# Embedding: two weight halves loaded together, and where their splits stand in ScalarE's queue

## The chip, the core and the metric

One NeuronCore of a Trainium2 chip runs the kernel. Its engines are TensorE (PE, matmuls), VectorE (DVE), ScalarE (ACT), GpSimd (POOL) and SyncE (SP), which issues nearly all of the DMAs. Each engine works through its own queue in order and waits on semaphores. The metric is the device time of one execution, in microseconds (us), as a median of several runs.

## What is computed

The reference is one layer of a hybrid encoder on 1024 tokens of 1024 channels in float32: an input layer norm, a gated-delta-net and a forgetting-attention group that read one combined projection, an output projection, an MLP, and between them residuals with layer norms. The part that the change touches is small, the per-layer embedding:

```python
ff = jnp.square(jax.nn.relu(h @ w_up[i])) @ w_down[i]
ple = (p[i] @ w_ple[i]) * jax.nn.sigmoid(h @ w_ple_gate[i] + b_ple_gate[i])
h = _layer_norm(ALPHA * h + ff + ple, ln2_g[i], ln2_b[i])
```

`p` has 1024 rows of 256 values and `w_ple` is 256 x 1024. Only the product `p @ w_ple` is made in the stage looked at here.

## The kernel before

Each float32 operand of a product is split in two parts that the matmul takes: `hi`, a rounded copy that ACT casts (`nc.scalar.copy`), and `lo`, the difference that DVE makes (`split_lo`, line 53). A product is then three matmuls, hi x hi, hi x lo and lo x hi, in one PSUM bank.

The kernel starts with the embedding because it needs nothing but inputs. `p` is loaded in two parts of 512 KB (`pt[:, 0:4]` and `pt[:, 4:8]`, lines 227 and 239). `w_ple` is loaded in two halves of 512 columns, 512 KB each, by `load_ple(n)` (line 229), which also issues the half's cast on ACT (line 234) and its difference on DVE (line 235). `ple_prep(half)` (line 262) transposes one part of `p` on PE, eight 128x128 transposes into two banks; ACT copies each bank into `pth` and DVE takes the difference into `ptl`. `ple_mm(t, n)` (line 272) makes one group of six matmuls for row group `t` and weight half `n` into a bank of a pool of three (`pj`), ACT evacuates the bank with a factor 0.5 (line 279), and SP stores the result in `ple_spill`. The order in the code is: transposes of the first part of `p`, four groups with half 0, transposes of the second part, four groups with half 1, then the eight groups of the second part.

In the same first stretch ACT and DVE split eight tiles of the value projection's weights (`load_wv`, tile `wvr`, lines 246 to 251, four buffers), a narrow tile `wv_s` is cast on DVE (line 284), and DVE makes the layer norm of the rows of `x` (`ln_rows`, line 133), three tiles of which are in flight. After the embedding PE goes through the eight row tiles: it transposes each normalised tile (`to_act`, line 151) and multiplies it with the value weights (line 309).

The order of instructions in each engine's queue is not that of the code. A planner runs the program through its own estimates of durations and landings, and on each engine gives the next place to the instruction that is ready by these estimates and stands earliest in the code. `tc.issue_after(ins)` pins what is traced in its block, as far as it runs on the engine of `ins`, behind `ins` in that engine's queue; instructions of other engines get no such edge. It adds no semaphore.

Of the kernel before, what the change touches and what calls it, by code (L numbers as in the profile page):

```python
# [32 lines left out]
def _sl(i, n=P):  # L33
    return slice(i * n, (i + 1) * n)
# [3 lines left out]
def tile_block(ctx: ExitStack, tc: tile.TileContext, x, p, ln_in_g, ln_in_b, w_in, conv_w, a_log, dt_bias,  # L38
               gdn_norm_g, b_f, fox_norm_g, w_out, ln1_g, ln1_b, w_up, w_down, w_ple, w_ple_gate,
               b_ple_gate, ln2_g, ln2_b, out):  # L40
    nc = tc.nc
    PS = bass.MemoryType.PSUM
    x, p, out = x[0], p[0, 0], out[0]
# [9 lines left out]
    def split_lo(eng, lo, src, hi):  # L53
        eng.tensor_tensor(out=lo, in0=src, in1=hi.bitcast(F32), op=ALU.subtract)  # L54
# [111 lines left out]
    def pj(name):  # L166

        return psd.tile([P, 512], F32, tag="pj", name=name)

    def sm(name):  # L170
        return psx.tile([P, 512], F32, tag="sm", name=name)
# [40 lines left out]
    with tc.tile_pool(name="start", bufs=2, reuse_waits="tile") as stp:  # L212
# [6 lines left out]
        def load_x(t):  # L219
            xts[t] = stp.tile([P, D], F32, tag="x", name=f"x{t}", bufs=3)  # L220
            nc.sync.dma_start(out=xts[t], in_=x[_sl(t), :])
# [7 lines left out]
        def load_ple(n):  # L229

            w = [wpool.tile([P, 2, 512], dt, tag=tag, name=f"{tag}_ple{n}")
                 for tag, dt in (("w_raw", F32), ("w_hi", F32R), ("w_lo", F32R))]
            nc.sync.dma_start(out=w[0], in_=w_ple[:, _sl(n, 512)].rearrange("(k q) c -> q k c", q=P))
            nc.scalar.copy(out=w[1], in_=w[0])
            split_lo(nc.vector, w[2], w[0], w[1])
            return w[1:]

        wpl = [load_ple(0)]
        nc.sync.dma_start(out=pt[:, 4:8], in_=pv[:, 4:8])
        load_x(0)  # L240
        wpl.append(load_ple(1))
        nc.gpsimd.dma_start(out=gb, in_=ln_in_g.partition_broadcast(P))
        nc.gpsimd.dma_start(out=bb, in_=ln_in_b.partition_broadcast(P))
        wvs = stp.tile([P, NK, 8], F32, name="wv_s", bufs=1)
# [17 lines left out]
        def ple_prep(half):  # L262
            for k in range(2):
                ps = sm("ps_pT")
                for i in range(4):
                    nc.tensor.transpose(ps[:, _sl(i)], pt[:, half * 4 + i, _sl(k)], ident)
                hi = pth[:, k, _sl(half, 512)]
                nc.scalar.copy(out=hi, in_=ps)
                lo = nc.vector.tensor_tensor(out=ptl[:, k, _sl(half, 512)], in0=ps, in1=hi.bitcast(F32), op=ALU.subtract)
            return lo.ins  # L270

        def ple_mm(t, n):
            so = stp.tile([P, 512], F32, tag="po", name="ple_o", bufs=5)
            ps = pj("ps_ple")
            wh, wl = wpl[n]
            for k in range(2):
                for wi, (aa, w) in enumerate(((pth, wh), (pth, wl), (ptl, wh))):
                    nc.tensor.matmul(ps, aa[:, k, _sl(t)], w[:, k], start=(k == 0 and wi == 0), stop=(k == 1 and wi == 2))
            nc.scalar.mul(out=so, in_=ps, mul=0.5)
            nc.sync.dma_start(out=ple_rows[t, :, _sl(n, 512)], in_=so)  # L280

        prep0 = ple_prep(0)
        with tc.issue_after(prep0):
            nc.vector.tensor_copy(out=wv_hi[:, :, 520:528], in_=wvs)
            split_lo(nc.vector, wv_lo[:, :, 520:528], wvs, wv_hi[:, :, 520:528])
        for t in range(4):
            ple_mm(t, 0)
        ple_prep(1)
        for t in range(4):
            ple_mm(t, 1)  # L290
        for n in range(2):
            for t in range(4, 8):
                ple_mm(t, n)
        for col in (512,):
            ahead[col] = proj_w(col)
        for t in range(NT):
# [8 lines left out]
            for n in range(2):  # L305
                ps = pj(f"psv{t}")
# [4 lines left out]
                cs, w = slice(264 * n, min(264 * n + 264, 512)), (264, 248)[n]  # L311
# [16 lines left out]
        ps = sm("ps_cols")  # L328
# [540 lines left out]
    n = len(steps)  # L869
# [117 lines left out]
    for t in range(NT):  # L987
# [6 lines left out]
        for n in range(2):  # L994
            ps = early.get((t, n))
            if ps is None:
                ps = pj("ps_mix")
# [423 lines left out]
    for js in ((0, 1), (2,), (3,)):  # L1421
        w = P * len(js)
# [13 lines left out]
        for j in js:  # L1436
            t = 4 + j
# [37 lines left out]
```

## Time and profile before

| | us |
|---|---|
| median of 3 runs (1410.28 to 1414.26) | 1412.11 |
| the profiled execution | 1411.87 |
| its span, first to last instruction | 1410.1 |
| PE busy | 1375.8 |
| DVE busy | 1084.5 |
| ACT busy | 559.3 |

The profile is of one execution. Start times are us from the first instruction. An entry in square brackets in a timeline is the idle time of the engine before the row, and what ended it. A time to landing runs from the issue of a DMA to its last byte. Matmul ends are modelled, so the steps between the starts of matmuls are a better measure than their durations.

### The profile page before, as it was taken

What the parts mean: (1) busy time and instruction counts of PE and PEld (TensorE: products, weight loads), DVE (VectorE), ACT (ScalarE), POOL (GpSimd) and SP (SyncE); (2) the same over time, 40 slices, a digit from 0 to 9 for tenths busy, and PEclk for the clock granted to TensorE, in tenths of its full rate; (3) what the DMA queues carried; (4) which work ended last, traced back from release to release, by engine and by line L of the source; (5) the groups of instructions that cost most, each with busy time, mean ns of one, the idle gap of its engine ahead of it and who ended that gap; (6) DMA issues with size and microseconds to landing.
All of it is one profiled execution on the core that took longest, in us unless ns stands there. A gap on an engine that the chain in (4) does not pass through costs nothing.

```text
span 1410.1 us, 20582 instructions
## 1 busy us (share of the span) xinstructions
PE 1375.8 (98%) x7342; PEld 1165.8 (83%) x7342; DVE 1084.5 (77%) x2273; ACT 559.3 (40%) x1044; POOL 15.4 (1%) x32
## 2 busy tenths in 40 slices
PE   7999999999999999999989999999999999999997
PEld 5997888988898887777889888888888888888885
DVE  6968899578566888968988766777666898748867
ACT  5323443243226767721133333333333444555421
POOL 1000000000000000000000000000000000000000
PEclk9999999999999999999999999999999999999999
DMA  9825434445478765234666744444446893334342
GB/s 304 282 104 180 150 83 116 146 157 149 127 190 199 172 150 166 68 133 168 214 215 207 237 137 153 157 160 147 148 131 228 315 342 111 97 97 125 117 134 83
DMA packets 193470, 232.74 MB, mean 165 GB/s; under 512 B 41638, under 2 KB 121687, under 8 KB 193367
## 3 DMA queue, kind: packets, MB, share of 16 engines
q1 hardware_dynamic: 187750, 226.69, 51.4%
q10 hardware_dynamic: 5232, 3.67, 1.0%
q8 instruction: 58, 0.95, 0.3%
q0 software_dynamic: 384, 1.06, 0.2%
q14 instruction: 46, 0.37, 0.1%
HBM read 155.29 MB, written 76.09 MB: 164 GB/s over the span
## 4 chain that ended last, share of the span: by engine, by line
PE 51%; DVE 3%; DMA 3%; issue 1%; SPq 0%; ACT 0%; DVEq 0%; ACTq 0%
PE ps_uP L1208 22%; PE ps_db L1328 9%; PE ps_da L1328 9%; PE ps_gP L1075 4%; PE ps_mix L954 3%; PE ps_db L1433 3%; DMA r<-t_spill 1%; DVE h L51 1%; PE ps_tr L961 1%; DMA h<-h_spill 0%; DMA wo_raw<-in_w_out_dram 0%; DMA hb<-h_spill 0%; DMA gA<-in_w_ple_gate_dram 0%; DMA h_spill<-h 0%; DVE gv L51 0%
## 5 line engine op out<-in xcount | busy, mean ns | idle before, releaser
L1208 PE MATMUL ps_uP<-T,uS 128*128 128x512 f32 x576 | 133.5, 390 | 0.0
L1208 PEld LDWEIGHTS ps_uP<-T,uS 128*128 128x128 f32 x576 | 108.1, 188 | 23.0
L1298 ACT CAST rh<-rr 128x512 fp32r<-128x512 f32 x112 | 69.9, 624 | 138.4 <-PE ps_db L1328 49.4
L54 DVE TENSOR_TENSOR rl<-rr,rh 128x512 fp32r<-128x512 f32 x112 | 77.1, 689 | 61.2 <-ACT rh L1298 22.3
L1208 PE MATMUL ps_uP<-B,uA 128*128 128x512 f32 x384 | 92.4, 396 | 0.0
L1208 PEld LDWEIGHTS ps_uP<-B,uA 128*128 128x128 f32 x384 | 72.2, 188 | 17.4
L954 PE MATMUL ps_mix<-wo,act_hi 128*128 128x512 f32 x256 | 81.7, 396 | 0.3 <-ACT act_hi L834 0.3
L207 PE MATMUL g<-act_hi,in_hi 128*128 128x512 f32 x192 | 75.5, 393 | 0.0
L207 PE MATMUL g<-act_hi,in_lo 128*128 128x512 f32 x192 | 75.3, 392 | 0.0
L207 PE MATMUL g<-act_lo,in_hi 128*128 128x512 f32 x192 | 74.9, 390 | 0.0
L54 DVE TENSOR_TENSOR uA<-uraw,uA 128x512 fp32r<-128x512 f32 x48 | 33.2, 691 | 47.8 <-ACT uA L1203 47.8
L1298 ACT CAST rl<-B 128x512 fp32r<-128x512 f32 x96 | 59.7, 623 | 24.5 <-PE ps_db L1328 11.5
L1203 ACT CAST uS<-wS 128x512 fp32r<-128x512 f32 x64 | 39.5, 624 | 73.0 <-issue 48.2
L54 DVE TENSOR_TENSOR ql<-B,rl 128x512 fp32r<-128x512 f32 x96 | 65.8, 686 | 0.3
L54 DVE TENSOR_TENSOR ptl<-ps_pt,pth 128x512 fp32r<-128x512 f32 (+2 forms) x96 | 51.1, 552 | 6.7 <-ACT pth L782 6.4
L954 PEld LDWEIGHTS ps_mix<-wo,act_hi 128*128 128x128 f32 x256 | 47.3, 188 | 10.1 <-DVE wo L54 0.6
L782 ACT CAST pth<-ps_pt 128x512 fp32r<-128x512 f32 (+2 forms) x96 | 44.4, 479 | 26.1 <-PE ps_pt L780 24.9
L51 DVE SCALAR_TENSOR_TENSOR cv<-g,hcw,cv 128x511 f32<-128x511 f32 (+2 forms) x72 | 52.8, 737 | 1.7 <-ACT cv L414 1.4
L764 ACT ACTIVATE s<-s,m 128x128 f32<-128x128 f32 (+3 forms) x64 | 49.9, 780 | 8.5 <-DVE m L761 7.8
L1328 PE MATMUL ps_db<-rl,rh 128*128 128x512 f32 x192 | 51.3, 389 | 0.0
L1328 PE MATMUL ps_db<-ql,rh 128*128 128x512 f32 x192 | 51.3, 389 | 0.0
L1328 PE MATMUL ps_db<-rl 128*128 128x512 f32 x192 | 51.3, 389 | 0.0
(358 smaller groups left out, 3586.0 us busy)
## 6 DMA issues: line engine op xcount, KB each, us to landing
uraw<-in_w_up_dram SPq DMA_DIRECT2D x32, 512.0 KB, 4.6
B<-in_w_down_dram SPq DMA_DIRECT2D x32, 512.0 KB, 5.1
rr<-rS SPq DMA_DIRECT2D x64, 256.0 KB, 2.6
in_raw<-in_w_in_dram SPq DMA_DIRECT2D x24, 512.0 KB, 4.3
rr<-rA SPq DMA_DIRECT2D x48, 256.0 KB, 2.8
h_spill<-h SPq DMA_DIRECT2D x16, 512.0 KB, 3.5
rA<-ub SPq DMA_DIRECT2D x32, 256.0 KB, 2.2
rS<-da SPq DMA_DIRECT2D x32, 256.0 KB, 2.1
```

What stands on the lines that cost most here:

```text
L51: nc.vector.scalar_tensor_tensor(out=o, in0=a, scalar=s, in1=b, op0=op0, op1=op1)
L54: eng.tensor_tensor(out=lo, in0=src, in1=hi.bitcast(F32), op=ALU.subtract)
L207: mm = nc.tensor.matmul(ps, w[:, k, :], a[n][:, :, k], start=(k == 0 and wi == 0), stop=(k == NK - 1 and wi == 2))
L764: nc.scalar.activation(out=s[:, :W], in_=s[:, :W], func=AF.Exp, bias=m[:, i:i + 1], scale=-1.0, accum_out=pairs[h // 2][2][:, r, j:j + 1])
L782: nc.scalar.copy(out=hi, in_=pt[:, :kn])
L954: nc.tensor.matmul(ps, a[t // 4][:, t % 4, k], w, start=(k == 0 and wi == 0), stop=(k == NK - 1 and wi == 2))
L1075: nc.tensor.matmul(ps[j // 2][:, j % 2], B[b][s][k][:, _sl(j)], a[w][:, k], start=(first and j % 2 == 0 and k == 0 and wi == 0), stop=(j % ...
L1203: nc.scalar.copy(out=hi, in_=a[s])
L1208: nc.tensor.matmul(ps[p], w[:, k], B[t][b][k], start=(chain is None and k == 0 and wi == 0), stop=(k == 3 and wi == 2), skip_group_check=c ...
L1298: nc.scalar.copy(out=hi, in_=src)
L1328: nc.tensor.matmul(ps[j], rs[x][:, _sl(j)], qs[y], start=(not chain and c == 0 and wi == 0), stop=(c == NP - 1 and wi == 2), skip_group_ch ...
L1433: nc.tensor.matmul(b[j], rs[x][:, i, _sl(j - js[0])], Q[c0 + i][y], start=(c0 == 0 and i == 0 and wi == 0), stop=(c0 + i == NP - 1 and wi ...
```

## The change

`load_ple` only loads now; a new `split_ple(n)` casts and subtracts. Both halves are loaded one behind the other, ahead of the second part of `p` and of the first tile of `x`. The split of half 0 is traced behind the first `ple_prep` and its cast is pinned in ACT's queue behind the second copy of the transposed `p` (`hi0`). The split of half 1 is traced behind the first four groups, its cast pinned behind the third evacuation (`o[2]`). The differences on DVE get no pin of their own. The same instructions run on the same data.

```diff
--- before.py
+++ after.py
@@ -231,14 +231,15 @@
             w = [wpool.tile([P, 2, 512], dt, tag=tag, name=f"{tag}_ple{n}")
                  for tag, dt in (("w_raw", F32), ("w_hi", F32R), ("w_lo", F32R))]
             nc.sync.dma_start(out=w[0], in_=w_ple[:, _sl(n, 512)].rearrange("(k q) c -> q k c", q=P))
-            nc.scalar.copy(out=w[1], in_=w[0])
-            split_lo(nc.vector, w[2], w[0], w[1])
-            return w[1:]
-
-        wpl = [load_ple(0)]
+            return w
+
+        def split_ple(n):
+            nc.scalar.copy(out=wpl[n][1], in_=wpl[n][0])
+            split_lo(nc.vector, wpl[n][2], wpl[n][0], wpl[n][1])
+
+        wpl = [load_ple(n) for n in range(2)]
         nc.sync.dma_start(out=pt[:, 4:8], in_=pv[:, 4:8])
         load_x(0)
-        wpl.append(load_ple(1))
         nc.gpsimd.dma_start(out=gb, in_=ln_in_g.partition_broadcast(P))
         nc.gpsimd.dma_start(out=bb, in_=ln_in_b.partition_broadcast(P))
         wvs = stp.tile([P, NK, 8], F32, name="wv_s", bufs=1)
@@ -265,26 +266,31 @@
                 for i in range(4):
                     nc.tensor.transpose(ps[:, _sl(i)], pt[:, half * 4 + i, _sl(k)], ident)
                 hi = pth[:, k, _sl(half, 512)]
-                nc.scalar.copy(out=hi, in_=ps)
+                last_hi = nc.scalar.copy(out=hi, in_=ps)
                 lo = nc.vector.tensor_tensor(out=ptl[:, k, _sl(half, 512)], in0=ps, in1=hi.bitcast(F32), op=ALU.subtract)
-            return lo.ins
+            return last_hi.ins, lo.ins
 
         def ple_mm(t, n):
             so = stp.tile([P, 512], F32, tag="po", name="ple_o", bufs=5)
             ps = pj("ps_ple")
-            wh, wl = wpl[n]
+            wh, wl = wpl[n][1:]
             for k in range(2):
                 for wi, (aa, w) in enumerate(((pth, wh), (pth, wl), (ptl, wh))):
                     nc.tensor.matmul(ps, aa[:, k, _sl(t)], w[:, k], start=(k == 0 and wi == 0), stop=(k == 1 and wi == 2))
-            nc.scalar.mul(out=so, in_=ps, mul=0.5)
+            o = nc.scalar.mul(out=so, in_=ps, mul=0.5)
             nc.sync.dma_start(out=ple_rows[t, :, _sl(n, 512)], in_=so)
-
-        prep0 = ple_prep(0)
+            return o.ins
+
+        hi0, prep0 = ple_prep(0)
+        with tc.issue_after(hi0):
+            split_ple(0)
         with tc.issue_after(prep0):
             nc.vector.tensor_copy(out=wv_hi[:, :, 520:528], in_=wvs)
             split_lo(nc.vector, wv_lo[:, :, 520:528], wvs, wv_hi[:, :, 520:528])
-        for t in range(4):
-            ple_mm(t, 0)
+        o = [ple_mm(t, 0) for t in range(4)]
+
+        with tc.issue_after(o[2]):
+            split_ple(1)
         ple_prep(1)
         for t in range(4):
             ple_mm(t, 1)
```

## Rows read from the trace of the kernel before

**Rows 1.** The page, part 1: busy time of each engine, its share, instructions.
```profile
PE 1375.8 (98%) x7342; PEld 1165.8 (83%) x7342; DVE 1084.5 (77%) x2273; ACT 559.3 (40%) x1044; POOL 15.4 (1%) x32
```

**Rows 2.** What PE waited for, whole span: total us, times, longest us.
```profile
PE ps_sc L756 <- DVE m L761: 2.0, 2, 1.4
...
PE ps_ple L278 <- ACT ple_o L279: 1.7, 2, 1.5
```

**Rows 3.** Timeline of PE, 0 to 27 us: start, duration, instruction, idle before.
```profile
5.49 1.94 PE L266 MATMUL ps_pT<-ident,p_raw 128*128 128x128 f32 x8 [5.49 <-DMA p_raw<-in_p_dram]
8.90 0.80 PE L278 MATMUL ps_ple<-w_hi_ple,pT_hi 128*128 128x512 f32 x1 [1.48 <-ACT pT_hi L268]
9.68 0.79 PE L278 MATMUL ps_ple<-w_lo_ple,pT_hi 128*128 128x512 f32 x1
...
11.01 0.63 PE L278 MATMUL ps_ple<-w_hi_ple,pT_hi 128*128 128x512 f32 x1
...
14.41 0.39 PE L278 MATMUL ps_ple<-w_hi_ple,pT_lo 128*128 128x512 f32 x1
...
15.81 0.40 PE L278 MATMUL ps_ple<-w_hi_ple,pT_lo 128*128 128x512 f32 x1
17.71 0.50 PE L278 MATMUL ps_ple<-w_hi_ple,pT_hi 128*128 128x512 f32 x1 [1.51 <-ACT ple_o L279]
18.05 0.39 PE L278 MATMUL ps_ple<-w_lo_ple,pT_hi 128*128 128x512 f32 x1
18.27 0.40 PE L278 MATMUL ps_ple<-w_hi_ple,pT_lo 128*128 128x512 f32 x1
...
20.00 0.47 PE L278 MATMUL ps_ple<-w_hi_ple,pT_hi 128*128 128x512 f32 x1
20.32 0.39 PE L278 MATMUL ps_ple<-w_lo_ple,pT_hi 128*128 128x512 f32 x1
```

**Rows 4.** Timeline of ACT, 0 to 21 us.
```profile
7.32 1.05 ACT L234 CAST w_hi_ple<-w_raw_ple 128x1024 fp32r<-128x1024 f32 x1 [5.24 <-DMA w_raw_ple<-in_w_ple_dram]
8.27 1.07 ACT L268 CAST pT_hi<-ps_pT 128x512 fp32r<-128x512 f32 x2
15.41 1.05 ACT L234 CAST w_hi_ple<-w_raw_ple 128x1024 fp32r<-128x1024 f32 x1 [6.07 <-DMA w_raw_ple<-in_w_ple_dram]
16.54 0.63 ACT L250 CAST wv_hi<-wvr 128x520 fp32r<-128x520 f32 x1
17.07 0.59 ACT L279 ACTIVATE ple_o<-ps_ple 128x512 f32<-128x512 f32 x1
...
19.61 1.10 ACT L279 ACTIVATE ple_o<-ps_ple 128x512 f32<-128x512 f32 x2
```

**Rows 5.** Timeline of SP's DMA issues, 0 to 21 us.
```profile
1.72 0.47 SPq L239 DMA_DIRECT2D p_raw<-in_p_dram  x1
...
2.77 0.56 SPq L233 DMA_DIRECT2D w_raw_ple<-in_w_ple_dram  x1
...
4.04 8.84 SPq L249 DMA_DIRECT2D wvr<-in_w_in_dram  x4
```

**Rows 6.** The tile w_raw of the embedding: its two loads' time to landing.
```profile
DMA to landing us min/median/max: 6.1/9.3/12.6
```

**Rows 7.** The tile p_raw, its load issued at 1.72: time to landing.
```profile
DMA to landing us min/median/max: 7.8/7.8/7.8
```

**Rows 8.** Busy us: length, PE, PEld, DVE, ACT, POOL; clock, DMA share, GB/s.
```profile
20.00:26.00 6.00, 5.83 (x27) 4.42 (x25) 6.00 (x12) 5.28 (x10) 0.00 (x0) 1.00 1.00 345
```

**Rows 9.** Timeline of DVE, 0 to 21 us.
```profile
15.86 0.20 DVE L284 CAST wv_hi<-wv_s 128x64 fp32r<-128x64 f32 x1 [4.89 <-DMA wv_s<-in_w_in_dram]
...
16.57 1.21 DVE L54 TENSOR_TENSOR w_lo_ple<-w_raw_ple,w_hi_ple 128x1024 fp32r<-128x1024 f32 x1
```

**Rows 10.** The tile wvr, its first load, issued at 4.04: time to landing.
```profile
DMA to landing us min/median/max: 12.5/12.5/12.5
```

**Rows 11.** Timeline of PE, 50 to 56 us: the one wait there.
```profile
54.69 0.39 PE L309 MATMUL psv<-wv_hi,act_lo 128*128 128x264 f32 x1 [0.88 <-DVE act_lo L54]
```

## The prediction

> **What bounds the kernel now.** First I read the busy shares of the page: TensorE (PE) works 98% of the span, VectorE (DVE) 77%, ScalarE (ACT) 40% [rows 1]. A stage is then worth what it takes from PE's idle time, so the second view is the list of what PE waited for. Only one entry there belongs to the embedding and to ACT's evacuations: 1.7 us in two waits, the longest 1.5 us [rows 2]. Nothing else that this diff touches can give more, unless the start of PE moves. So the stake is 1.5 us of 1410, about 0.1%.
>
> The third view is the timeline of PE over the first 27 us [rows 3]. The first product of the embedding starts at 8.90. [...] At 15.81 the last matmul of the third row group starts, then PE stands 1.51 us until 17.71: the fourth group needs one of three PSUM banks, and the bank's evacuation is late.
>
> The ACT timeline says why [rows 4]. ACT runs its queue in order. The cast of the second weight half (w_hi of half 1) stands in the queue ahead of the first evacuation, and sits 6.07 us until its data lands at 15.41; it takes 1.05 us, a cast of wvr follows at 16.54, and only then, at 17.07, comes the evacuation that PE waits for. The load was issued at 2.77 [rows 5] and needed 12.6 us to land, while the load of half 0 needed 6.1 [rows 6]: it stood behind the second half of p and x0.
>
> **The change part by part.**
> *Load order.* The load of half 1 moves ahead of two transfers of 512 KB each on SP's queue. In the old order half 1 landed at 2.77 + 12.6 = 15.4; in the new one it lands between half 0 (7.3) and the time that the second half of p took until now, 1.72 + 7.8 = 9.5 [rows 6, 7]. That half of p slips by one transfer: 0.52 MB at 345 GB/s [rows 8] is 1.5 us, so 11.0. PE reads it after its fourth group, which started at 17.71, and before 20.00 [rows 3]: over 6 us of cover. x0 slips as much, to 15.4 at the latest, the old landing of half 1; DVE reads it right behind the cast that waits for wv_s at 15.86 [rows 9]. The bytes ahead of wv_s and of wvr are the same, so neither moves. Cost of the load order: 0 (0.5 us if x0 is later than I bound it).
>
> *Split of half 0 behind the transposes' copies.* Until now ACT did w_hi at 7.32, on its landing, and the two copies from 8.27; the first product started at 8.90 [rows 3, 4]. Reversed, the two copies (1.07 us) run while the transposes end at about 7.43, the second from 7.4 to 8.0, and w_hi from 8.0 to 9.0. The first matmul then starts at 9.05, w_lo (1.22 us on DVE) ends at 10.2, and the second matmul starts at 10.2 instead of 9.68. The third no longer waits: until now it and its follower stood apart by DVE's copy, and the fourth started at 11.01; now the fourth starts at 10.2 + 2 x 0.43 = 11.1. Net +0.1 us, between -0.3 and +0.5.
>
> *Split of half 1 behind the third evacuation.* What it removes: ACT no longer sits until 15.41. What the diff doesn't say is where the casts of wvr stand against the evacuations; the planner chooses that by its own estimates. In the trace of before, one wvr cast stands ahead of the first evacuation. wvr's first tile was issued at 4.04 [rows 5] and landed 12.5 us later, at 16.5 [rows 10]; its cast starts at 16.54 [rows 4]. So this cast was no longer waiting for ACT but for its data, and if it stays ahead of the first evacuation, **the new wait ends where the old one did**: evacuation at 17.07, PE at 17.71, gain 0. If it falls behind the evacuation, that can run when the first group is done, before 13, and PE goes on at 16.2: gain 1.5.
>
> What it adds: w_hi of half 1 (1.05 us) and its w_lo (1.22 us) now stand behind the third evacuation. On ACT the stretch from 16.54 is full: a cast of wvr, the first evacuation at 17.07, four more pieces (three casts and the second evacuation), and the third evacuation, which starts at 19.61 [rows 4]. That one takes 0.55, so w_hi runs from 20.2 to 21.2 and w_lo on DVE from 21.2 to 22.5. PE needs them for the first group of half 1, whose first matmul started at 20.00 and the second at 20.32 [rows 3]. With w_lo at 22.5 PE is up to 2.1 us late there. If the first evacuation goes early ACT is 0.55 ahead and PE 1.6 late. Neither engine has room to hide it: between 20 and 26 us DVE is busy 6.00 of 6.00 and ACT 5.28 [rows 8]. w_lo used to lie at 16.57 [rows 9], where DVE now has nothing before the casts of wvr, so its 1.2 us are pushed into DVE's full stretch. Everything behind it on DVE, the layer norm and the release of the x tiles, comes up to 1.2 us later.
>
> Where it is given back: PE waits for DVE once more, 0.88 us at 54.69 [rows 11]; a late PE loses part of its lateness there, if DVE is not late as well. Of 1.6 to 2.1 us at most 0.9 is taken back, so the bounds are 0.7 and 2.1. I take **+1.2 us**, the time by which DVE is late, since from that wait on PE goes at DVE's pace.
>
> Sum: the profiled execution took 1411.87 us, 1410.1 of span and 1.8 around it; 0 for the loads, +0.1 and +1.2 give 1413.2. The median of three, 1412.11, is 0.2 above it, so in its terms 1413.4; I forecast 1413.3.
>
> [...]
>
> **The rivals.**
> 1. *Gain.* The planner puts all three evacuations and w_hi of half 1 ahead of the wvr casts. Then w_hi runs at about 16.9 to 17.9, PE ends group four at 17.6, the transposes at 18.4, and the first group of half 1 starts its second matmul at 19.2: 1.1 to 1.5 us early. For: the evacuations can be ready from 13 on, wvr not before 16.54. Against: the casts of wvr then start 1.4 us later, DVE's splits of them too, and DVE's full stretch returns it at 54.69. Time 1410.6 to 1412.
> 2. *Exchange of waits, no effect.* The wvr cast stays first and PE fills the wait for w_lo with other ready groups (the second half of p with half 0). 1412.1.
> [...]
> 4. *Another plan.* The planner orders every queue from these times on; a shift of 1 us at the start can rearrange the projections after it. Past the start no entry in the list of PE's waits has more than 2.0 us in sum [rows 2]; two or three such entries more or fewer are 4 to 6 us either way.
>
> **How the numbers follow.** Forecast, 0.5 to 2.1 us slower: 0.45. Rival 1: 0.25. Rival 2: 0.13. Rival 3: 0.05. Rival 4: 0.12, both signs alike. About 0.3%, 4.2 us, is what a measurement of this kernel can tell from no change; the runs shown lie 4 us apart. Only rival 4 clearly passes that bound, and rival 3 lies on it, so half of its 0.05 counts: slower 0.08, faster 0.05, within 0.3% 0.87. Range: rival 1 less 1.5 us of scatter of the median, 1409, and rival 3, 1417; outside lies most of rival 4.
>
> **What would show it.** Load order: half 1 landing before 10 us, wv_s still at 15.9. First split: first matmul at 9.0 to 9.1, second at 10.2. Second split: no ACT idle ended by half 1's load. Whether the first evacuation stands ahead of the first wvr cast decides between forecast and gain: an evacuation near 13 and PE without the 1.5 us gap. Forecast: a PE wait for w_hi or w_lo of half 1 at 20 to 22.5. Rival 1: that wait missing, half 1 begun before 19, and a longer wait at 54.7. [...] Wrong outright: new PE waits after 60 us of over 4 us in sum.

## The result: 13 us slower, all of it lost before 106 us

| | before | after |
|---|---|---|
| median, us | 1411.34 | 1424.55 |
| the profiled execution, us | 1411.87 | 1423.72 |
| its span, us | 1410.1 | 1422.0 |
| first product of the embedding starts, us | 8.90 | 18.27 |
| last product of the embedding ends, us | 37.44 | 48.63 |
| last product with the value weights ends, us | 93.81 | 106.30 |
| last product of the MLP ends (`ps_db`), us | 1401.04 | 1412.87 |

(With one more run of before its median is 1411.34, not 1412.11.) The ratio is 1.0092, with a 95% interval of 1.0076 to 1.0109. The medians lie 13.2 us apart, the two profiled executions 11.9. The lower rows of the table say where the time lies: the first product is 9.4 us late, the end of the embedding 11.2, the value products 12.5, and from there to the end of the MLP's last product the distance stays between 10.6 and 12.8 us, wherever the two traces are compared.

What PE waited for in the changed kernel (total us, times, longest us). The lines answer to [rows 2]:

```profile
PE ps_pT L267 <- DMA p_raw<-in_p_dram: 10.9, 2, 5.6
PE ps_ple L279 <- ACT w_hi_ple L237: 3.7, 2, 3.4
...
PE ps_ple L279 <- ACT ple_o L280: 1.4, 1, 1.4
...
PE ps_ple L279 <- DVE w_lo_ple L54: 1.0, 1, 1.0
```

The wait for evacuations that I wanted gone, 1.7 us, is 1.4. New are 3.7 us for w_hi, 1.0 us for w_lo, and 5.3 us in which the transposes of the second half of p wait for its data.

The timeline of ACT answers to [rows 4]:

```profile
6.74 0.59 ACT L269 CAST pT_hi<-ps_pT 128x512 fp32r<-128x512 f32 x1 [4.66 <-PE ps_pT L267]
7.59 0.59 ACT L269 CAST pT_hi<-ps_pT 128x512 fp32r<-128x512 f32 x1 [0.27 <-PE ps_pT L267]
16.65 0.62 ACT L251 CAST wv_hi<-wvr 128x520 fp32r<-128x520 f32 x1 [8.47 <-DMA wvr<-in_w_in_dram]
17.18 1.04 ACT L237 CAST w_hi_ple<-w_raw_ple 128x1024 fp32r<-128x1024 f32 x1
18.12 1.68 ACT L251 CAST wv_hi<-wvr 128x520 fp32r<-128x520 f32 x3
...
22.09 0.60 ACT L280 ACTIVATE ple_o<-ps_ple 128x512 f32<-128x512 f32 x1 [1.32 <-PE ps_ple L279]
...
25.58 0.60 ACT L280 ACTIVATE ple_o<-ps_ple 128x512 f32<-128x512 f32 x1 [0.76 <-PE ps_ple L279]
26.07 1.04 ACT L237 CAST w_hi_ple<-w_raw_ple 128x1024 fp32r<-128x1024 f32 x1
```

The two copies of p run as soon as PE has transposed, at 6.74 and 7.59. Both halves of w_ple had landed long before ACT went on: SP issued their loads at 1.23 and about 1.7, and they needed 5.9 and 8.6 us, so half 0 was in by about 7.1 and half 1 by about 10.3.

```profile
1.23 0.94 SPq L233 DMA_DIRECT2D w_raw_ple<-in_w_ple_dram  x2
DMA to landing us min/median/max: 5.9/7.2/8.6
```

Yet ACT sits 8.47 us, because the next place in its queue is not w_hi of half 0 but **a cast of wvr**, whose data lands at 16.65. Only at 17.18 comes w_hi.

PE over the same stretch, to be read against [rows 3]:

```profile
5.62 1.94 PE L267 MATMUL ps_pT<-ident,p_raw 128*128 128x128 f32 x8 [5.62 <-DMA p_raw<-in_p_dram]
12.86 1.97 PE L267 MATMUL ps_pT<-ident,p_raw 128*128 128x128 f32 x8 [5.30 <-DMA p_raw<-in_p_dram]
18.27 1.65 PE L279 MATMUL ps_ple<-w_hi_ple,pT_hi 128*128 128x512 f32 x3 [3.44 <-ACT w_hi_ple L237]
...
27.16 0.72 PE L279 MATMUL ps_ple<-w_hi_ple,pT_hi 128*128 128x512 f32 x2 [0.22 <-ACT w_hi_ple L237]
29.24 0.50 PE L279 MATMUL ps_ple<-w_hi_ple,pT_hi 128*128 128x512 f32 x1 [1.35 <-ACT ple_o L280]
30.78 0.51 PE L279 MATMUL ps_ple<-w_lo_ple,pT_hi 128*128 128x512 f32 x1 [1.04 <-DVE w_lo_ple L54]
...
31.37 0.63 PE L279 MATMUL ps_ple<-w_hi_ple,pT_hi 128*128 128x512 f32 x1
...
34.77 0.39 PE L279 MATMUL ps_ple<-w_lo_ple,pT_hi 128*128 128x512 f32 x1
```

The second transposes now stand ahead of the first product and wait until 12.86 for the second half of p; then PE waits 3.44 us more for w_hi. The first product starts at 18.27. At half 1 there are three waits in a row, 0.22, 1.35 and 1.04 us, and from 31.37 to 34.77 eight steps of 0.43 us.

DVE, against [rows 9]:

```profile
17.30 0.70 DVE L54 TENSOR_TENSOR wv_lo<-wvr,wv_hi 128x520 fp32r<-128x520 f32 x1 [8.40 <-ACT wv_hi L251]
17.92 0.18 DVE L288 CAST wv_hi<-wv_s 128x64 fp32r<-128x64 f32 x1
18.25 1.23 DVE L54 TENSOR_TENSOR w_lo_ple<-w_raw_ple,w_hi_ple 128x1024 fp32r<-128x1024 f32 x1
...
29.51 1.22 DVE L54 TENSOR_TENSOR w_lo_ple<-w_raw_ple,w_hi_ple 128x1024 fp32r<-128x1024 f32 x1
```

The cast of wv_s comes later than before, at 17.92, since it stands behind a difference of wvr, and the difference of half 0 stands behind both. The difference of half 1 runs at 29.51.

### The profile page after: what moved, and what is told of

Read it like the earlier page. It is cut to its first block, busy times and chain, and to the rows that moved or that the text cites. A ratio compares the mean times of both kernels' runs of the same rounds, so it can differ in the third digit from the quotient of the medians.

```text
span 1422.0 us, 20588 instructions
## 1 busy us (share of the span) xinstructions
PE 1378.3 (97%) x7342; PEld 1166.5 (82%) x7342; DVE 1084.1 (76%) x2273; ACT 558.6 (39%) x1044; POOL 15.3 (1%) x32
## 4 chain that ended last, share of the span: by engine, by line
PE 52%; DMA 2%; DVE 1%; issue 0%; SPq 0%; ACT 0%; DVEq 0%; ACTq 0%
PE ps_uP L1214 22%; PE ps_db L1334 9%; PE ps_da L1334 9%; PE ps_mix L960 5%; PE ps_gP L1081 3%; PE ps_db L1439 3%; DMA r<-t_spill 1%; PE ps_tr L967 1%; DMA gA<-in_w_ple_gate_dram 0%; DMA wo_raw<-in_w_out_dram 0%; DMA hb<-h_spill 0%; DVE gv L51 0%; DVE r L48 0%; DVE acc L51 0%; DVE t L48 0%
## 5 line engine op out<-in xcount | busy, mean ns | idle before, releaser
L54 DVE TENSOR_TENSOR rl<-rr,rh 128x512 fp32r<-128x512 f32 x112 | 76.9, 687 | 60.2 <-ACT rh L1304 22.5
```

## The experiments

Theory Q: a cast of wvr, waiting for data until 16.6, stands ahead of half 0 in ACT's queue, and that is the loss. Rivals: the load order (L), and the split of half 1 behind the third evacuation (S). All diffs are against the changed kernel.

### One part of the change undone at a time

**old_loads** puts the load order back:

```diff
-        wpl = [load_ple(n) for n in range(2)]
+        wpl = [load_ple(0)]
         nc.sync.dma_start(out=pt[:, 4:8], in_=pv[:, 4:8])
         load_x(0)
+        wpl.append(load_ple(1))
```

> Only the load order goes back (half 1 behind the second half of p and x0); both splits stay where the change puts them. Theory Q: the first product still waits for a cast behind wvr and starts at about 18.3 us, 1422 to 1427 us. Rival L: 1411 to 1414 us.

Measured: 1424.53 us, ratio 1.0079 (1.0060 to 1.0098). The first product starts at 18.05, behind the same two rows on ACT, a cast of wvr at 16.43 and w_hi at 16.96. The load order carries none of the loss; rival L falls. (PE's second transposes had their data at 9.46 here, against 12.86, and it made no difference, since w_hi came later still. What a late second half of p costs when w_hi is early is in split1_back and wvr_late below.)

**split0_back** puts the split of half 0 back ahead of the casts of wvr:

```diff
         wpl = [load_ple(n) for n in range(2)]
+        split_ple(0)
...
-        with tc.issue_after(hi0):
-            split_ple(0)
```

> Only the split of half 0 goes back to its place ahead of the casts of wvr; the load order and the split of half 1 behind the third evacuation stay. Theory Q: first product at 8.9 us; half 1 is up to 2 us late, so 1411 to 1415 us. Rival S (the loss lies in the split of half 1 behind the third evacuation, with PE's gaps and the lower clock after them): 1420 us or more.

Measured: 1415.56 us beside 1413.01 of before, ratio 1.0016 (1.0006 to 1.0026), 2.3 us. ACT and PE of this kernel:

```profile
16.66 0.62 ACT L252 CAST wv_hi<-wvr 128x520 fp32r<-128x520 f32 x1 [7.40 <-DMA wvr<-in_w_in_dram]
17.19 0.59 ACT L281 ACTIVATE ple_o<-ps_ple 128x512 f32<-128x512 f32 x1
...
19.73 0.60 ACT L281 ACTIVATE ple_o<-ps_ple 128x512 f32<-128x512 f32 x1
20.21 1.05 ACT L237 CAST w_hi_ple<-w_raw_ple 128x1024 fp32r<-128x1024 f32 x1
```

```profile
8.82 0.80 PE L280 MATMUL ps_ple<-w_hi_ple,pT_hi 128*128 128x512 f32 x1 [1.24 <-ACT pT_hi L270]
...
17.83 0.50 PE L280 MATMUL ps_ple<-w_hi_ple,pT_hi 128*128 128x512 f32 x1 [2.39 <-ACT ple_o L281]
...
21.32 1.00 PE L280 MATMUL ps_ple<-w_hi_ple,pT_hi 128*128 128x512 f32 x3 [0.96 <-ACT w_hi_ple L237]
23.20 0.80 PE L280 MATMUL ps_ple<-w_lo_ple,pT_hi 128*128 128x512 f32 x1 [0.89 <-DVE w_lo_ple L54]
```

The first product is back at 8.82. So of 13.2 us about 11 go with the place of half 0's split, and 2.3 remain with half 1's. The rows also show what was predicted for half 1 alone: the evacuation still runs behind the first cast of wvr, at 17.19 (before: 17.07), PE's gap ahead of the fourth group stays (it ends at 17.83, before at 17.71; PE comes to it earlier, so it is 2.39 us long), w_hi of half 1 runs at 20.21, and PE gets w_lo at 23.20. Rival S holds for about a sixth of the loss (0.8 to 3.7 us by the interval).

**split1_back** puts the split of half 1 back instead, ahead of the casts of wvr:

```diff
         load_x(0)
+        split_ple(1)
...
-        with tc.issue_after(o[2]):
-            split_ple(1)
```

> Only the split of half 1 goes back ahead of the casts of wvr; the split of half 0 stays behind the transposes' copies. Theory Q: the first product starts at about 18 us as in the changed kernel and the waits of PE for half 1 at 27 to 31 us are gone, 1420 to 1424 us. Rival S: 1411 to 1414 us.

Measured: 1417.40 us, ratio 1.0035 (1.0025 to 1.0045), and the first product at 14.46, not 18. My expectation missed, for the planner made another order. ACT:

```profile
10.72 1.04 ACT L237 CAST w_hi_ple<-w_raw_ple 128x1024 fp32r<-128x1024 f32 x1 [8.64 <-DMA w_raw_ple<-in_w_ple_dram]
11.68 1.06 ACT L270 CAST pT_hi<-ps_pT 128x512 fp32r<-128x512 f32 x2
12.63 1.06 ACT L237 CAST w_hi_ple<-w_raw_ple 128x1024 fp32r<-128x1024 f32 x1
16.27 0.62 ACT L252 CAST wv_hi<-wvr 128x520 fp32r<-128x520 f32 x1 [2.58 <-DMA wvr<-in_w_in_dram]
```

w_hi of half 1 now comes first and waits for its own data until 10.72, the copies of p wait behind it, and w_hi of half 0 got its place ahead of the first cast of wvr. Half 0 is there at 13.7; PE, whose second transposes wait for p until 12.84, starts the product right behind them. The split of half 0 is pinned as in the changed kernel, but what stands ahead of it is not.

**loads_only** has the new load order alone, with both splits traced ahead of the casts of wvr, half 1's behind the load of x0:

```diff
         wpl = [load_ple(n) for n in range(2)]
+        split_ple(0)
         nc.sync.dma_start(out=pt[:, 4:8], in_=pv[:, 4:8])
         load_x(0)
+        split_ple(1)
...
-        with tc.issue_after(hi0):
-            split_ple(0)
...
-        with tc.issue_after(o[2]):
-            split_ple(1)
```

> Both halves loaded first as in the change, but each split is traced ahead of the casts of wvr, as before the change. Theory Q (a cast of wvr that waits for its data until 16.5 us stands ahead of the cast of half 0 on ACT, and everything starts 9.4 us late): the first product starts at 8.9 us again, the cast of half 1 runs near 9 to 10 us, the time is 1409 to 1412 us. Rival L (the load order delays the second half of p, x0 and what follows): the time stays at 1420 us or more.

Measured: 1415.35 us, ratio 1.0015 (1.0001 to 1.0030), 2 us slower than before (0.1 to 4.2 by the interval), where I expected 1409 to 1412 us and the first product at 8.9. On ACT the cast of half 1, waiting for its data until 10.67, stands ahead of the copies of p, and the first product starts at 12.25, 3.35 us late. It is the mechanism of theory Q with another load in the part of wvr.

### Does the start follow wvr's landing?

**wvr_late_pin** loads the second tile of x ahead of wvr, and pins half 0 behind the first cast of wvr, as the planner had put it (`wv_casts` collects the casts of wvr):

```diff
+        load_x(1)
         load_wv(0)
-        load_x(1)
...
-        with tc.issue_after(hi0):
+        with tc.issue_after(hi0), tc.issue_after(wv_casts[0]):
             split_ple(0)
```

> As the kernel with wvr late, but the cast of half 0 is pinned behind the first cast of wvr, as it stood in the changed kernel. Theory Q: the first product follows wvr's landing, which comes one x tile (0.52 MB at some 330 GB/s, 1.6 us) later: first product at about 19.9 us instead of 18.3; 1425 to 1431 us.

Measured: 1424.35 us, ratio 1.0088 (1.0072 to 1.0104). ACT, then PE:

```profile
18.84 0.62 ACT L253 CAST wv_hi<-wvr 128x520 fp32r<-128x520 f32 x1 [2.96 <-DMA wvr<-in_w_in_dram]
19.37 1.04 ACT L237 CAST w_hi_ple<-w_raw_ple 128x1024 fp32r<-128x1024 f32 x1
```

```profile
13.28 1.97 PE L269 MATMUL ps_pT<-ident,p_raw 128*128 128x128 f32 x8 [5.87 <-DMA p_raw<-in_p_dram]
20.47 1.65 PE L281 MATMUL ps_ple<-w_hi_ple,pT_hi 128*128 128x512 f32 x3 [5.21 <-ACT w_hi_ple L237]
```

The cast of wvr moved from 16.65 to 18.84, 2.19 us, where one x tile was estimated at 1.6 (at some 330 GB/s; before's trace has 326 from 8.9 to 37.3 us); the first product from 18.27 to 20.47, 2.20 us. The start follows the landing one to one. The total did not follow, and lies below the 1425 to 1431 us that I expected: PE waits 1.97 us more for w_lo of half 0, but at half 1 only 0.23 and 0.26 us, where the changed kernel had 2.6 us of waits and then steps of 0.43 us, so the embedding ends at 48.7, beside 48.6.

**wvr_late** is the same without that pin.

> The changed kernel with the load of the second x tile issued ahead of wvr's first four. By its estimates the planner then puts the cast of half 0 ahead of the casts of wvr on ACT; PE's second transposes stay ahead of the first product, and on DVE the cast of wv_s stays ahead of the difference of half 0. Theory Q2: though wvr lands later, the first product comes earlier, at 14.5 us, bound by the second half of p, and the first matmul with w_lo at 17.9; 1416 to 1422 us. A theory by which any delay of the loads makes it slower: 1425 us or more.

Measured: 1422.37 us, ratio 1.0078 (1.0053 to 1.0102), just above the 1416 to 1422 expected. ACT, then PE:

```profile
7.68 1.05 ACT L237 CAST w_hi_ple<-w_raw_ple 128x1024 fp32r<-128x1024 f32 x1
...
18.68 2.58 ACT L251 CAST wv_hi<-wvr 128x520 fp32r<-128x520 f32 x4 [3.19 <-DMA wvr<-in_w_in_dram]
```

```profile
14.52 1.63 PE L279 MATMUL ps_ple<-w_hi_ple,pT_hi 128*128 128x512 f32 x3
18.66 0.50 PE L279 MATMUL ps_ple<-w_lo_ple,pT_hi 128*128 128x512 f32 x1 [2.52 <-DVE w_lo_ple L54]
...
28.08 1.65 PE L279 MATMUL ps_ple<-w_hi_ple,pT_hi 128*128 128x512 f32 x3 [4.26 <-ACT w_hi_ple L237]
```

wvr lands later and the first product starts **earlier**, at 14.52, behind the second transposes, because the planner put half 0 ahead of the casts of wvr. (That it did so because it takes wvr to come later is my reading of its rule; its estimates are not in the traces.) The difference of half 0, behind the cast of wv_s on DVE, let PE go on at 18.66 (expected 17.9; wv_s landed at 16.7). Half 1's cast now stands behind all eight casts of wvr and PE waits 4.26 us for it, until 28.08, so the embedding ends at 47.9 all the same. The order of the queue, not the transfer, is what half 0 suffers from.

### Taking away what stands ahead

**act_freed** traces the casts of wvr and their differences (`split_wv`, four tiles at a time) behind the third evacuation and pins them there; the second transposes are pinned on PE behind the fourth group. The loads of wvr's last four tiles and of the third x tile come later in the code with them:

```diff
...
-                nc.scalar.copy(out=wv_hi[:, k, 0:520], in_=raw)
-                split_lo(nc.vector, wv_lo[:, k, 0:520], raw, wv_hi[:, k, 0:520])
...
         with tc.issue_after(o[2]):
             split_ple(1)
-        ple_prep(1)
+            split_wv(0)
+        load_wv(4)
+        with tc.issue_after(o[2]):
+            split_wv(4)
+        load_x(2)
+        with tc.issue_after(mms[3]):
+            ple_prep(1)
```

> The changed kernel with its pins, but the casts of wvr are traced and pinned behind the third evacuation, and the transposes of the second half of p are pinned on PE behind the fourth group. So nothing that waits for wvr stands ahead of half 0 on ACT. Theory Q1 (ACT's queue alone carries the loss): the first product starts at 9.0 us, its w_lo matmuls at 10.2, 1411 to 1414 us. Theory Q2 (DVE's queue has a second trap: the difference of half 0 now stands behind the cast of wv_s, which waits for its data until 15.9): the first product starts at 9.0, but its first matmul with w_lo only at about 17.9 us, 1418 to 1424 us.

Measured: 1418.62 us beside 1412.65, ratio 1.0034 (1.0021 to 1.0048). PE, then DVE:

```profile
9.22 1.65 PE L282 MATMUL ps_ple<-w_hi_ple,pT_hi 128*128 128x512 f32 x3 [1.62 <-ACT w_hi_ple L237]
17.97 0.80 PE L282 MATMUL ps_ple<-w_lo_ple,pT_hi 128*128 128x512 f32 x1 [7.10 <-DVE w_lo_ple L54]
```

```profile
15.99 0.20 DVE L293 CAST wv_hi<-wv_s 128x64 fp32r<-128x64 f32 x1 [7.04 <-DMA wv_s<-in_w_in_dram]
16.10 0.69 DVE L130 BATCH_NORM_STATS2 st<-x 128x6 f32<-128x512 f32 x1
16.71 1.21 DVE L54 TENSOR_TENSOR w_lo_ple<-w_raw_ple,w_hi_ple 128x1024 fp32r<-128x1024 f32 x1
```

The first product starts at 9.22, does three matmuls with w_hi, and then PE stands **7.10 us** for w_lo: on DVE the difference of half 0 stands behind the cast of wv_s, which waits for its data until 15.99. Theory Q2 is right on the place (17.97, expected 17.9), a second queue with a second trap. On the total it was too high (1418 to 1424 expected, some 7 to 13 us above before; it is 4.8 by the ratio): from 17.97 to the end of the embedding PE has no wait here, where the changed kernel has 2.6 us.

**both_freed** pins the cast of wv_s and the first layer norm behind the difference of half 0 as well:

```diff
         with tc.issue_after(hi0):
-            split_ple(0)
-        with tc.issue_after(prep0):
+            lo0 = split_ple(0)
+        with tc.issue_after(lo0):
             nc.vector.tensor_copy(out=wv_hi[:, :, 520:528], in_=wvs)
...
-            with tc.issue_after(prep0) if t == 0 else ExitStack():
+            with tc.issue_after(lo0) if t == 0 else ExitStack():
```

> As the kernel with ACT freed, and on DVE the cast of wv_s and the first layer norm are pinned behind the difference of half 0 instead of behind the copies of p. Theory Q2: first product at 9.0, first matmul with w_lo at 10.2, no gap ahead of the fourth group, and half 1 waits for its w_lo, which stands on DVE behind the statistics of the third x tile (landing near 20 us), until about 21 to 22 us: 1411 to 1415 us. Theory Q1 makes no difference between this kernel and the one before it.

Measured: 1417.01 us, ratio 1.0031 (1.0020 to 1.0042), 4.4 us.

```profile
9.13 1.65 PE L282 MATMUL ps_ple<-w_hi_ple,pT_hi 128*128 128x512 f32 x3 [1.62 <-ACT w_hi_ple L237]
...
22.96 0.79 PE L282 MATMUL ps_ple<-w_lo_ple,pT_hi 128*128 128x512 f32 x1 [4.87 <-DVE w_lo_ple L54]
```

Half 0 is now as planned, PE goes from 9.13 through four groups and the transposes without the gap of 1.5 us, and then waits 4.87 us for w_lo of half 1, which on DVE stands behind statistics of x tiles and starts at 21.73. The loss has moved to half 1, as expected, but is larger than the 1411 to 1415 that I gave it.

**dve_freed** moves the pin on DVE alone and leaves ACT as in the changed kernel (its diff is the one printed for both_freed).

> The changed kernel with one pin moved: on DVE the cast of wv_s and the first layer norm are pinned behind the difference of half 0. ACT's order is that of the changed kernel, with the first cast of wvr ahead of half 0. Theory Q2 (two queues, each holds half 0 by itself to about the same time): the first product stays at 18.3 us, nothing is gained, 1422 to 1427 us. A theory that DVE's queue is the one that counts: first product and time return towards those before the change.

Measured: 1420.22 us beside 1411.64, ratio 1.0058 (1.0042 to 1.0074). The first product is at 18.29 as expected: ACT's queue by itself holds half 0. But 4.8 us come back further on, which I had not expected: PE's waits for half 1 are 0.23 and 0.54 us instead of 2.6, no step after 28 us is over 0.4 us, and the embedding ends at 44.3 instead of 48.6.

The start and the total do not go together, then. With the first product at 18.29 (dve_freed) the ratio is 1.0058, at 14.52 (wvr_late) it is 1.0078, at 9.13 (both_freed) 1.0031: what half 0 gets back is in part lost again at half 1, when something else stands ahead of that. The runs give the price of half 0's place as a whole, about 11 us (split0_back); they do not split it among the three queues.

### Both halves early

**all_early** keeps the loads of the change and takes every instruction that waits for wvr off the way: half 0 split as before the change, half 1 pinned behind the second copy of p, the casts of wvr behind the third evacuation, the second transposes behind the fourth group:

```diff
         wpl = [load_ple(n) for n in range(2)]
+        split_ple(0)
...
         hi0, prep0 = ple_prep(0)
         with tc.issue_after(hi0):
-            split_ple(0)
+            split_ple(1)
...
         with tc.issue_after(o[2]):
-            split_ple(1)
+            split_wv(0)
```

> Both halves loaded first; the split of half 0 where it was before the change, the split of half 1 pinned behind the second copy of p, the casts of wvr behind the third evacuation, the second transposes behind the fourth group. No instruction that PE needs before 20 us stands behind one that waits for wvr or wv_s, but for w_lo of half 1 (DVE, 16.6 to 17.9). Theory Q2: first product at 8.9 us, no PE gap over 0.5 us up to 30 us, embedding 1.5 us shorter; what DVE gives back later decides between 1409 and 1412 us. If the loss were in the load order, 1415 us or more.

Measured: 1413.16 us beside 1412.65, ratio 1.0005 (0.9995 to 1.0014): no difference that can be told, and not the gain that 1409 to 1412 us would have been.

```profile
8.74 0.79 PE L283 MATMUL ps_ple<-w_hi_ple,pT_hi 128*128 128x512 f32 x1 [1.24 <-ACT pT_hi L273]
...
25.03 0.50 PE L283 MATMUL ps_ple<-w_hi_ple,pT_lo 128*128 128x512 f32 x1 [0.68 <-DVE pT_lo L274]
...
36.34 0.50 PE L283 MATMUL ps_ple<-w_hi_ple,pT_hi 128*128 128x512 f32 x1 [1.51 <-ACT ple_o L285]
```

PE goes without a gap from 8.74 to 24, and the wait ahead of the fourth group is gone. It pays 0.68 us (I expected no gap over 0.5) at 25.03 for a difference of p on DVE and 1.51 us at 36.34 for an evacuation, which on ACT stood behind the cast of `in_raw` until 34.74. The embedding ends at 38.0, where before it was 37.4. So the 1.5 us for which a change here can play are not to be had by this order either: they are given back within the embedding.

## Why the prediction was wrong

**The stake: right; the loads: no cost, though two landings were put too early.** No run was faster than before, and all_early shows that even the 1.5 us is given back. The load order cost nothing beside the late w_hi (old_loads). But half 1 landed at about 10.3, not between 7.3 and 9.5, and the second half of p at 12.8, not 11.0. wv_s and wvr stay where they were (wv_s in at 16.0, before at 15.9; first cast of wvr at 16.65, before at 16.54).

**The step that failed: the split of half 0 behind the transposes' copies**, put at +0.1 us, between -0.3 and +0.5. I placed w_hi at 8.0, straight behind the second copy, as if the pin gave it that place. A pin says behind what an instruction stands, not what else may stand between. Tracing the split behind `load_wv` also put all casts of wvr earlier in the code than half 0, and the planner gave one of them the next place on ACT: w_hi ran at 17.18, not 8.0. Why it took that cast to be ready first, no run shows. It cost 9.4 us at the first product. Where nothing stands ahead, the times of this step come out: in both_freed w_hi runs at 8.03 and the first product starts at 9.13. The pieces were in the prediction: I asked where the casts of wvr stand against the evacuations, and had their landing at 16.5, but never asked it against half 0, which had moved past the same casts. Nor did I ask it for the other two queues that the move touches: on DVE the difference of half 0 fell behind the cast of wv_s (act_freed: 7.10 us by that alone), and on PE the second transposes went ahead of the first product (wvr_late: not before 14.52 by that alone). For them I had counted "over 6 us of cover", which holds only while they stay behind the fourth group.

**The split of half 1 behind the third evacuation: right in mechanism and about right in size.** Alone (split0_back) it cost 2.3 us (0.8 to 3.7 by the interval), where I had +1.2 with bounds 0.7 and 2.1; the value lies above the upper bound, the interval covers it. The six steps of 0.43 us behind the waits (23.80 to 26.36) take some 1.2 us more than at 0.23, which my sum did not hold. The evacuation came at 17.19 behind wvr, "the new wait ends where the old one did"; w_hi at 20.21 against 20.2 predicted; w_lo at 23.20 against 22.5. In the changed kernel the same part costs 2.61 us of waits at half 1.

**The clock: it fell at half 1, and the forecast had no term for that.** The granted clock in the changed kernel:

```profile
29.00:31.30 2.30, 1.03 (x3) 0.66 (x4) 2.30 (x4) 0.18 (x1) 0.00 (x0) 1.00 0.82 252
31.30:34.40 3.10, 3.10 (x9) 2.36 (x9) 3.10 (x9) 0.60 (x1) 0.00 (x0) 0.50 0.02 5
```

(columns as in [rows 8]). Before the fall PE had stood 1.35 us, done one matmul, and stood 1.04 us. The eight steps from 31.37 to 34.77 took 3.40 us; at 0.23 us each, the step from 24.68 to 26.54 where the column reads 1.00, they take 1.86: 1.5 us. In split0_back one gap of 2.39 us was followed by steps of 0.24 us and less from 18.16 on (granted clock 1.00 from 18.00 to 21.00), and the two waits of 0.96 and 0.89 us, with three matmuls between, were followed by six steps of 0.43 (0.50 from 23.20 to 26.40). Behind long single gaps the slow step came too: 4.26 us in wvr_late (at 28.08) and 4.87 us in both_freed (at 22.96) were each followed by steps of 0.43 us. So in these runs the length of one gap doesn't decide by itself.

The step of 0.43 us in the sum for half 0 is in before's timeline of PE, eight times from 11.01 to 14.41, and six steps of 0.23 follow:

```profile
11.44 0.63 PE L278 MATMUL ps_ple<-w_lo_ple,pT_hi 128*128 128x512 f32 x1
11.86 0.63 PE L278 MATMUL ps_ple<-w_hi_ple,pT_lo 128*128 128x512 f32 x1
...
14.64 0.39 PE L278 MATMUL ps_ple<-w_hi_ple,pT_hi 128*128 128x512 f32 x1
14.87 0.40 PE L278 MATMUL ps_ple<-w_lo_ple,pT_hi 128*128 128x512 f32 x1
```

The upper end of the range, 1417 for rival 3, rested on an estimate of 2.6 us, thirteen steps of 0.43 instead of 0.23 us behind one gap of 2.3 us; no run shows that. In the changed kernel eight such steps stand behind two waits of 1.35 and 1.04 us and cost 1.5 us; in split0_back six stand behind 0.96 and 0.89 us and cost 1.2.

The sum for the embedding: 9.4 us of late start; then 2.61 us of waits and 1.5 us of low clock at half 1, less before's waits of 1.7 and some 0.8 us of transposes that now lie in the late start, is +1.6, and the table has +1.8 (11.2 less 9.4). In the value products another 1.3 us are lost, of which 0.7 is in PE's waits there (1.6 us instead of 0.9); the rest I can't name from the rows.

**Rivals 1 and 2** did not come: PE neither started half 1 early nor filled its waits with groups of the second half of p; ahead of w_lo of half 1 it did three matmuls with w_hi (27.16 and 29.24). For rival 1 all_early shows that its gain would have been returned.

**Rival 4**, another plan later on, explains nothing: behind 106 us the distance to before moves by about 2 us in both directions and ends where it began, within 1 us. By the two lists of PE's waits, those new or longer behind 106 us sum to some 4.1 us, those gone or shorter to some 3.7. So the sign "new PE waits after 60 us of over 4 us in sum" was met, and yet says nothing: the waits gone have to be counted with it.

**The chances.** Slower by over 0.3% had 0.08. All cases were built on one order of ACT's queue around half 0, and the order was the unknown. A bound from both sides was at hand in the rows: w_hi of half 0 at 8.0 or, behind a cast of wvr, at 17.2, that is 0 or +9. How likely the one or the other was, the rows of before don't say; split1_back and wvr_late, which keep the pin and get half 0 ahead of wvr, show how little decides it.

## What to carry to other kernels

An instruction that is moved later in the code can be passed by everything that it is moved behind, on each engine that its step uses: list for every queue which of those wait for a load, and when that load really lands. A pin in a queue is a lower bound for one instruction on one engine; if the place matters, pin what must not come ahead of it too, and check the other engines of the same step. When only the estimate of a planner decides between two orders, the price of the wrong one belongs in the range.

## What the runs showed of the hardware

In the changed kernel the steps between matmuls are 0.43 us from 19.72 to 24.41, while the granted-clock column reads 1.00 from 18.27 to 24.41; the later steps of 0.43 us in the same execution, from 31.37 to 34.77, stand beside 0.50 (31.30 to 34.40). Before's first steps of 0.43 us, from 11.01 to 14.41, stand beside 1.00 as well. So in these two traces the spacing shows the first slow stretch and the column does not. And no long gap stood ahead of every slow stretch: in split0_back waits of 0.96 and 0.89 us, with three matmuls between, were followed by steps of 0.43 us, and a gap of 2.39 us a little earlier by steps of 0.24 us and less.
